# Two more pauses in the merge of the dilated branches of a hybrid decoder kernel

## The chip, the cores and the metric

One core of a Trainium2 chip runs the whole program. The metric is device time in microseconds (us) from launch to end; for the kernel before the median of three runs is given, and beside it one further execution that the hardware profiler recorded.

## The reference, cut to what matters

Two residual layers work on x of 2048 rows by 1024 columns. The change lies in layer 1, a dilated sliding-window attention with 16 heads of 64 columns. Each of its branches gives, for every query, an output `o`, the lowest score `m` and the sum `l` of its exponentials; the branches are then mixed by their softmax denominators:

```python
for o_i, m_i, l_i in branches:
    w_i = l_i * jnp.exp(m_i - big_m)
    num = num + w_i * o_i.astype(jnp.float32)
    den = den + w_i
return (num / den).astype(v.dtype)
...
oc = merge_heads(dilated_mixture(q, k, v)) * jax.nn.silu(gc)
return jnp.einsum('bse,ed->bsd', oc, w_out)
```

## The kernel before, in words

The kernel folds the three branches of the reference into two (`br` 0 and 1: near keys with a mask that counts some of them twice, and keys at stride 16). `dilated()` runs through 8 pairs of heads `p`, and in each through 4 chunks `c` of 512 queries, 2 halves of a chunk and the 2 branches: 16 units for a pair, 128 in all. A unit has scores on TensorE (L1268, tile `s_ps`), a mask and row minimum on VectorE (L1276, into `P` and the statistics `st`), exponentials on ScalarE (L1278), transposes of P on TensorE (L709, `t_ps`), their copies to SBUF on VectorE and ScalarE (L713, `pt`), and the product with the values on TensorE (L1309, `o_ps`). Scores are written four slots ahead of the rest. After the second half of a chunk ScalarE copies `o_ps` to a tile `or` (L1312); there are 11 `or` buffers, and a pair fills 8.

When a pair is complete its merge begins, spread over the units of the next pair. `merge()` returns a list of functions; entry i runs at the start of unit i + 1 after the pair's last unit, and `None` leaves a unit without a step:

- `rows`: TensorE transposes the statistics (L1334, `x_ps`), ScalarE copies them to `rt` (L1337), and SyncE's queue (SP) writes `rt` to DRAM in four transfers (`std`).
- `columns`: nine transfers on the same queue bring them back in another layout, as tile `W`.
- `weights`: nine small VectorE operations and one ScalarE exponential (L1355 `mm`, L1356 `E`, L1357, L1358 `W`, L1359 to L1361, L1363 and L1364 `w`).
- `expand(0)`, `expand(1)`: two GpSimd operations each (L1370) spread the weights into tile `X`.
- `chunk(c, br)`: TensorE spreads X over the heads (L1378, `bc_ps`, which takes one of the three PSUM buffers of the scores), VectorE multiplies `or` by it (L1379); for branch 1 GpSimd adds the two branches (L1385) and multiplies by the gate (L1386), and SP stores the result (`og`). The gate tile `sg` is loaded by branch 0's chunk.

For pairs 0 to 5, which the change touches, the list has 14 entries, for pairs 6 and 7 another. The first merge (of pair 0, run during pair 1) is called M1 below, and so on to M6; M7 is pair 6's.

The order in which each engine gets its instructions isn't the order of these lists: a scheduler of the framework sorts them by the program's order and by when it expects operands and buffers to be free, engine by engine, DMA queues included. A pause can so move instructions that the diff doesn't name. Each engine then runs its own list strictly in that order.

Of the kernel before, what the change touches and what calls it, by code (L numbers as in the profile page):

```python
# [83 lines left out]
def trunk(ctx: ExitStack, tc: tile.TileContext, A, out):  # L84
# [6 lines left out]
    def dma(o, i):  # L91
        if o.dtype == F32R:
            o = o.bitcast(F32)
        if i.dtype == F32R:
            i = i.bitcast(F32)
        return queue[0].dma_start(o, i)  # L96
# [7 lines left out]
    def dap(t, off, ap):  # L104
        return bass.AP(tensor=t.tensor, offset=t.offset + off, ap=ap)
# [1040 lines left out]
    def dilated():  # L1146
# [88 lines left out]
        def unit(p, c, br, half):  # L1235
# [81 lines left out]
            if (br, half) == (1, 1):  # L1317
                if p == 7:
                    what = merge(p, c, 1)
                elif c == 3:  # L1320
                    what = merge(p, 0, 4)
# [3 lines left out]
        def merge(p, c0, n):  # L1325

            box = {}
            R = 8 * n
            sd = st_d[p + c0]

            def rows():

                ps = x_bank("x_ps")
                TE.transpose(ps[0:4 * R, 0:128],  # L1334
                             stats[p][:, c0:c0 + n].rearrange("p c x b h t -> p (c x b h t)"), ident)
                rt = ap2.tile([128, 128], F32, tag="rt", name="rt", bufs=2)
                SC.copy(rt[0:4 * R], ps[0:4 * R, 0:128])  # L1337
                for c in range(n):
                    dma(dap(sd, c * 512, [[n * 512, 8], [128, 4], [1, 128]]), rt[32 * c:32 * c + 32])

            def columns():

                box["W"] = W = ap2.tile([128, 2, 2, 128], F32, tag="W", name="W", bufs=1)
                dma(W[0:R, :, 0], dap(sd, 0, [[128, R], [2 * R * 128, 2], [1, 128]]))
                for k in range(2):
                    for t in range(4):
                        dma(W[0:R, k, 1, 32 * t:32 * t + 32],
                            dap(sd, (2 * k + 1) * R * 128 + 128 * t, [[512, 2 * n], [32, 4], [1, 32]]))

            def weights():  # L1350
                W = box["W"][0:R]
                m, l = W[:, 0], W[:, 1]
                mm = ap2.tile([128, 128], F32, tag="mm", name="mm", bufs=1)[0:R]
                E = ap2.tile([128, 2, 128], F32, tag="E", name="E", bufs=1)[0:R]
                V.tensor_tensor(mm, m[:, 0], m[:, 1], OP.min)  # L1355
                V.tensor_tensor(E, mm[:, None, :].to_broadcast([R, 2, 128]), m, OP.subtract)  # L1356
                SC.activation(E, E, AF.Exp)  # L1357
                V.tensor_tensor(l, l, E, OP.mult)  # L1358
                V.tensor_tensor(mm, l[:, 0], l[:, 1], OP.add)  # L1359
                V.reciprocal(mm, mm)  # L1360
                V.tensor_tensor(E, E, mm[:, None, :].to_broadcast([R, 2, 128]), OP.mult)  # L1361
                ws = [ap2.tile([128, 2, 128], F32R, tag=f"w{k}", name=f"w{k}", bufs=1)[0:R] for k in range(2)]
                V.tensor_copy(ws[0], E)  # L1363
                V.tensor_tensor(ws[1], E, ws[0].bitcast(F32), OP.subtract)  # L1364
                box["w"] = ws

            def expand(br):

                for k in range(2):
                    PO.tensor_tensor(X[64 * br + 32 * k:64 * br + 32 * k + R].rearrange("p (r y) -> p r y", r=4),  # L1370
                                     box["w"][k][:, br, None, :].bitcast(F32).to_broadcast([R, 4, 128]),
                                     cc[0:R, C_M4:C_M4 + 4, None].to_broadcast([R, 4, 128]), OP.mult)

            def chunk(c, br):
                o = outs[p, br, c]
                bc = x_bank("bc_ps")
                bs = slice(64 * br, 64 * br + 64)
                TE.matmul(bc, sels[2 + c if n == 4 else 6][bs], X[bs], start=True, stop=True)  # L1378
                V.tensor_tensor(o, bc, o, OP.mult)  # L1379
                if br == 0:  # L1380
                    gates[p, c] = ap2.tile([128, 512], F32, tag="sg", name="sg", bufs=4)
                    dma(gates[p, c], sg_d[1][p, :, 512 * c:512 * c + 512])
                    return
                eng = V if (p, c) == (7, 3) else PO
                eng.tensor_tensor(o, o, outs[p, 0, c], OP.add)  # L1385
                eng.tensor_tensor(o, o, gates[p, c], OP.mult)  # L1386
                dma(og_d[1][c][p], o)

            if p < 6:
                fs = [rows, columns, None, weights, lambda: expand(0), lambda: expand(1)]  # L1390
                fs += [lambda c=c, br=br: chunk(c, br) for c in range(4) for br in range(2)]
            else:
                fs = [rows, columns] + [None] * (c0 < 3) + [weights, lambda: (expand(0), expand(1))]
                fs += [lambda c=c: (chunk(c, 0), chunk(c, 1)) for c in range(c0, c0 + n)]
            return [(i + 1, f) for i, f in enumerate(fs) if f]
# [72 lines left out]
```

## Time and profile before

| what | value |
|---|---|
| median of 3 runs | 3220.56 us (3219.57 to 3225.43) |
| the profiled execution | 3230.95 us, of it 3228.9 us span |
| TensorE busy | 3080.9 us |
| VectorE, ScalarE, GpSimd busy | 1567.0, 1282.1, 511.9 us |
| mean granted TensorE clock | 0.968 of full speed |

The span is the time from the first to the last recorded instruction. Busy time is the union of an engine's instructions; "idle before" is the time in which an engine had nothing running before an instruction, with what released it. A granted clock of 1.00 is 2.4 GHz and 0.50 is 1.2 GHz. The dilated attention lies between about 2503 and 3060 us of the span.

### The profile page before, as it was taken

What the parts mean: (1) busy time and instruction counts of PE and PEld (TensorE: products, weight loads), DVE (VectorE), ACT (ScalarE), POOL (GpSimd) and SP (SyncE); (2) the same over time, 40 slices, a digit from 0 to 9 for tenths busy, and PEclk for the clock granted to TensorE, in tenths of its full rate; (3) what the DMA queues carried; (4) which work ended last, traced back from release to release, by engine and by line L of the source; (5) the groups of instructions that cost most, each with busy time, mean ns of one, the idle gap of its engine ahead of it and who ended that gap; (6) DMA issues with size and microseconds to landing.
All of it is one profiled execution on the core that took longest, in us unless ns stands there. A gap on an engine that the chain in (4) does not pass through costs nothing. (4 is left out here: it accounts for less than half of the span.)

```text
span 3228.9 us, 60884 instructions
## 1 busy us (share of the span) xinstructions
PE 3080.9 (95%) x24252; PEld 2517.8 (78%) x24252; DVE 1567.0 (49%) x4176; ACT 1282.1 (40%) x2954; POOL 511.9 (16%) x495
## 2 busy tenths in 40 slices
PE   7999999999999999999999999999999888888898
PEld 6978889987777777777777998888888777767687
DVE  6443421001777788888554402311100777767643
ACT  5311111112766656556442321111111867766321
POOL 3200100002333200000032202220000022123321
PEclk9999999999999999999999999999999999987799
DMA  7255542216222221211352324674314655553252
GB/s 263 84 177 188 174 149 86 72 63 224 101 74 101 74 93 64 76 55 65 99 179 96 131 86 139 202 217 142 113 66 144 182 173 176 178 156 119 92 175 98
DMA packets 272309, 415.27 MB, mean 129 GB/s; under 512 B 28172, under 2 KB 155788, under 8 KB 267032
## 3 DMA queue, kind: packets, MB, share of 16 engines
q1 hardware_dynamic: 268712, 399.58, 38.6%
q0 software_dynamic: 3312, 11.80, 1.2%
q8 instruction: 190, 3.11, 0.4%
q14 instruction: 95, 0.78, 0.1%
HBM read 259.23 MB, written 152.05 MB: 127 GB/s over the span
## 5 line engine op out<-in xcount | busy, mean ns | idle before, releaser
L246 PE MATMUL pj<-hl,wh 128*128 128x512 f32 x1536 | 389.8, 396 | 0.0
L246 PE MATMUL pj<-hh,wh 128*128 128x512 f32 x1536 | 389.2, 395 | 0.0
L246 PE MATMUL pj<-hh,wl 128*128 128x512 f32 x1536 | 388.9, 395 | 0.0
L834 PE MATMUL s_ps<-K,Q 64*128 64x512 f32 (+2 forms) x1920 | 338.2, 395 | 19.0 <-DVE P L843 15.0
L709 PE MATMUL t_ps<-cc,P 64*128 64x64 f32 x5536 | 314.4, 236 | 33.5 <-DVE pt L713 20.4
L246 PEld LDWEIGHTS pj<-hl,wh 128*128 128x128 f32 x1536 | 289.4, 189 | 69.0 <-issue 0.5
L246 PEld LDWEIGHTS pj<-hh,wl 128*128 128x128 f32 x1536 | 288.6, 188 | 68.6 <-issue 0.5
L854 ACT ACTIVATE P<-P,m 128x1664 f32<-128x1664 f32 (+15 forms) x256 | 306.8, 1200 | 87.8 <-DVE m L849 87.6
L246 PEld LDWEIGHTS pj<-hh,wh 128*128 128x128 f32 x1536 | 288.1, 188 | 68.3 <-issue 1.0
L709 PEld LDWEIGHTS t_ps<-cc,P 64*128 64x128 f32 x5536 | 245.2, 143 | 114.3 <-issue 61.0
L923 PEld LDWEIGHTS o_ps<-pt,v 128*64 128x64 f32 (+1 forms) x3264 | 253.8, 158 | 87.2 <-issue 52.9
L923 PE MATMUL o_ps<-pt,v 128*64 128x128 f32 (+1 forms) x3264 | 317.1, 286 | 2.9 <-ACT pt L713 2.7
L1278 ACT ACTIVATE P<-P,st 128x256 f32<-128x256 f32 (+3 forms) x512 | 266.9, 524 | 92.0 <-DVE st L1276 90.6
L713 ACT COPY pt<-t_ps 128x512 f32<-128x512 f32 (+7 forms) x448 | 213.3, 495 | 176.2 <-PE t_ps L709 163.7
L231 DVE TENSOR_TENSOR wl<-w,wh 128x512 fp32r<-128x512 f32 (+1 forms) x128 | 84.9, 705 | 405.2 <-ACT wh L230 405.2
L713 DVE COPY pt<-t_ps 128x512 f32<-128x512 f32 (+5 forms) x384 | 229.9, 609 | 87.8 <-PE t_ps L709 69.0
L1276 DVE CUSTOM_DVE_ANT_0 P<-s_ps,band 128x256 f32<-128x256 f32 (+3 forms) x512 | 204.6, 448 | 111.4 <-PE s_ps L1268 108.3
L834 PEld LDWEIGHTS s_ps<-K,Q 64*128 64x128 f32 x1920 | 202.4, 192 | 60.6 <-DVE P L843 24.9
L1268 PE MATMUL s_ps<-K,Q 64*128 64x256 f32 (+2 forms) x1536 | 193.6, 339 | 12.9 <-DVE st L1276 11.5
L1309 PE MATMUL o_ps<-pt,v 128*64 128x128 f32 x2272 | 178.6, 298 | 9.4 <-DMA v<-v 3.5
L267 ACT ACTIVATE hi<-pj 128x512 fp32r<-128x512 f32 x80 | 47.8, 597 | 350.0 <-PE pj L246 329.8
L840 DVE CUSTOM_DVE_ANT_0 P<-s_ps,F 128x512 f32<-128x512 f32 (+1 forms) x192 | 121.4, 669 | 109.7 <-PE s_ps L834 108.9
(245 smaller groups left out, 4371.6 us busy)
## 6 DMA issues: line engine op xcount, KB each, us to landing
Q<-q SPq DMA_DIRECT2D x31, 1024.0 KB
ada<-ada_w SPq DMA_DIRECT2D x96, 256.0 KB
sg<-t2k SPq DMA_DIRECT2D x64, 256.0 KB
xt<-x SPq DMA_DIRECT2D x32, 512.0 KB
w<-w SPq DMA_DIRECT2D x64, 256.0 KB
q<-yb SPq DMA_DIRECT2D x64, 256.0 KB
x<-x SPq DMA_DIRECT2D x28, 512.0 KB
w<-w0b SPq DMA_DIRECT2D x56, 256.0 KB
```

The lines of the kernel that those rows point to most:

```text
L231: V.tensor_tensor(wl[:, 2 * q:2 * q + 2, :n], w[:, :, :n], wh[:, 2 * q:2 * q + 2, :n].bitcast(F32), OP.subtract)
L246: TE.matmul(ps, a[:, d, 128 * j:128 * j + 128], b[:, d, :], start=n == 0, stop=n == 23)
L709: TE.transpose(ps[k][:, n], b[rs], ident[rs, rs])
L713: last_flip[eng is SC] = f(pt[:, :len(blocks), 64 * k:64 * k + 64], ps[k][:, :len(blocks)])
L834: TE.matmul(ps[j][:, :n], queries[p, i // 4][hs, a, qs], keys[p][b][hs, c0:c0 + n], start=first, stop=a == 1)
L840: V.tensor_tensor_reduce(P[:, c0:c0 + n], ps[j][:, :n], forgets[p][j][:, c0:c0 + n], 1.0, 3.0e38, OP.add, OP.min, m)
L854: SC.activation(P, P, AF.Exp, bias=lows[j], scale=-1.0, accum_out=lt[:, j, col:col + 1])
L923: TE.matmul(o[:, cs], values[p][:, b, hs], pts[j, b], start=b == 0, stop=b == i)
L1268: TE.matmul(ps[hh][:, o:o + N], q[hs, qs], t["keys"](kk[hs]), start=k == 0, stop=k == 2)
L1276: V.tensor_tensor_reduce(P[:, hh, j, :n], ps[hh][:, o:o + n], m[:, m.shape[1] - n:], 1.0, 3.0e38, OP.add, OP.min, mn)
L1278: SC.activation(P[:, hh, j, :n], P[:, hh, j, :n], AF.Exp, bias=mn, scale=-1.0, accum_out=l)
L1309: TE.matmul(to, values[p, br][:, kc, hs], where[hh, j, o, kc], start=k == 0, stop=k == n - 1)
```

## The change

For pairs 0 to 5 the list of the merge gets two more `None`. The one behind the first `None` sets `weights` and all that follows one unit later; the one after `expand(1)` sets the chunks one unit later again, two in all. The list has 16 entries in place of 14. Nothing is computed otherwise.

```diff
             if p < 6:
-                fs = [rows, columns, None, weights, lambda: expand(0), lambda: expand(1)]
+                fs = [rows, columns, None, None, weights, lambda: expand(0), lambda: expand(1), None]
                 fs += [lambda c=c, br=br: chunk(c, br) for c in range(4) for br in range(2)]
```

What the scheduler makes of it, at three places. First TensorE in M1, in the stretch after the transposes that stand beside the statistics (`s_ps` scores, `t_ps` transposes, `o_ps` products with the values, `bc_ps` the spread weights). Before:

```order
L709 MATMUL t_ps<-cc,P 128x64 x16
L1309 MATMUL o_ps<-pt,v 64x4x32 x8
L709 MATMUL t_ps<-cc,P 128x64 x16
L1309 MATMUL o_ps<-pt,v 64x128 x7
L1378 MATMUL bc_ps<-X,sel_1700 128x512
L1268 MATMUL s_ps<-K,Q 128x256 x12
```

With the change, from the same row on:

```order
L709 MATMUL t_ps<-cc,P 128x64 x16
L1268 MATMUL s_ps<-K,Q 128x256 x12
L1309 MATMUL o_ps<-pt,v 64x4x32 x8
L709 MATMUL t_ps<-cc,P 128x64 x16
L1268 MATMUL s_ps<-K,Q 128x384 x6
L1309 MATMUL o_ps<-pt,v 64x128 x8
L1378 MATMUL bc_ps<-X,sel_1700 128x512
```

Two groups of scores that stood behind the first `bc_ps` now stand ahead of it. All rows ahead of this place are the same; M2 to M6 change in the same way.

Second VectorE in M1, at the end of `weights` (`w` are its two results, L1276 the masks of the scores):

```order
 L713 COPY pt<-t_ps 128x8x64
 L1361 TENSOR_TENSOR E<-E,mm 32x256
-L1363 CAST w_25768<-E 32x256
-L1364 TENSOR_TENSOR w_25769<-E,w_25768 32x256
+L1363 CAST w_25818<-E 32x256
+L1276 ISA P,st<-s_ps,band 128x256
+L1276 ISA st 128x1
+L1364 TENSOR_TENSOR w_25819<-E,w_25818 32x256
+L1276 ISA P,st<-s_ps,band 128x256
```

The first operation of `weights`, L1355, keeps its place on VectorE in all six merges (the same row number in both lists); only the end of `weights` moves, by one mask of a score, and the first L1379, which stood some rows behind it, moves further down.

Third SP's queue between M1 and M2 (`og_3` the last result of M1, `v` values for a later pair, `std` the statistics of M2):

```order
 L96 DMA og_3_79<-or 128x512
-L96 DMA K<-k_67 128x1024
-L96 DMA Q<-q_66 128x2048
-L96 DMA sg<-sg_71 128x512
-L96 DMA Q<-q_66 128x2048
 L96 DMA v<-v_69 128x16x128
-L96 DMA v<-v_69 32x4x128
 L96 DMA std_89<-rt 8x4x128 x4
```

The store of M1's last result now stands right ahead of the large load of `v`, which stands ahead of M2's `std`; one small load of `v` that stood there now comes behind. It is the same ahead of M3 to M6; ahead of M1 nothing moves.

## Rows read from the trace of the kernel before

**Rows 1.** The page's busy time of each engine: time, share of the span, instructions.

```profile
PE 3080.9 (95%) x24252; PEld 2517.8 (78%) x24252; DVE 1567.0 (49%) x4176; ACT 1282.1 (40%) x2954; POOL 511.9 (16%) x495
```

**Rows 2.** Windows from one transpose of the statistics to the next, M4 to M6.

```profile
core 0: us, PE busy (x) PEld busy (x) DVE busy (x) ACT busy (x) POOL busy (x), PEclk, DMA share, GB/s
...
2749.00:2810.00 61.00, 53.90 (x776) 44.39 (x772) 48.53 (x174) 44.29 (x152) 14.62 (x12) 0.92 0.56 174
2810.00:2880.00 70.00, 61.22 (x777) 49.92 (x773) 48.25 (x172) 44.98 (x152) 14.56 (x12) 0.83 0.50 153
2880.00:2948.00 68.00, 59.65 (x769) 48.19 (x765) 47.44 (x171) 45.56 (x152) 14.57 (x12) 0.85 0.45 134
```

**Rows 3.** Waits of PE, 2560 to 2950 us: who, for whom, total us, times, longest.

```profile
PE t_ps L709 <- DVE pt L713: 19.7, 8, 4.5
PE bc_ps L1378 <- POOL X L1370: 10.1, 6, 2.7
...
PE t_ps L709 <- ACT pt L713: 5.0, 6, 1.6
```

**Rows 4.** Waits of DVE in the same stretch.

```profile
DVE or L1379 <- PE bc_ps L1378: 23.4, 14, 3.1
DVE mm L1355 <- DMA W<-std: 23.3, 6, 5.7
```

**Rows 5.** Timeline of M1: start, duration, instruction, idle before it.

```profile
2576.89 0.28 DVE L1355 TENSOR_TENSOR mm<-W 32x128 f32<-32x128 f32 x1 [2.96 <-DMA W<-std]
...
2578.64 0.71 PE L709 MATMUL t_ps<-cc,P 64*128 64x64 f32 x15 [2.40 <-DVE pt L713]
...
2582.49 0.71 PE L709 MATMUL t_ps<-cc,P 64*128 64x64 f32 x15 [1.64 <-ACT pt L713]
...
2583.43 4.51 POOL L1370 TENSOR_TENSOR X<-w,cc 32x512 fp32r<-32x512 f32 x4 [80.69 <-DVE w L1363]
...
2586.88 0.79 PE L1378 MATMUL bc_ps<-X,sel 64*128 64x512 f32 x1 [2.67 <-POOL X L1370]
...
2587.71 0.69 DVE L1379 TENSOR_TENSOR or<-bc_ps,or 128x512 f32<-128x512 f32 x1 [2.78 <-PE bc_ps L1378]
```

**Rows 6.** Timeline from the end of M1 to the start of M2.

```profile
2611.32 0.40 PE L1378 MATMUL bc_ps<-X,sel 64*128 64x512 f32 x1
...
2616.34 0.32 SPq L96 DMA_DIRECT2D og<-or  x1
...
2618.79 0.96 PE L1268 MATMUL s_ps<-K,Q 64*128 64x256 f32 x12
...
2623.54 5.97 SPq L96 DMA_DIRECT2D v<-v  x2
...
2625.60 0.33 PE L1334 MATMUL x_ps<-cc,st 128*128 128x128 f32 x1
...
2627.71 0.26 ACT L1337 COPY rt<-x_ps 128x128 f32<-128x128 f32 x1
...
2629.60 2.91 SPq L96 DMA_DIRECT2D std<-rt  x4
2632.56 1.61 SPq L96 DMA_DIRECT2D v<-v  x3
2634.88 5.82 SPq L96 DMA_DIRECT2D W<-std  x9
```

**Rows 7.** Windows at low granted clock, in M1 to M6 (columns as in Rows 2).

```profile
2584.00:2592.00 8.00, 5.33 (x46) 4.04 (x44) 3.98 (x13) 2.04 (x8) 4.53 (x5) 0.57 0.50 164
...
2838.00:2854.00 16.00, 16.00 (x108) 12.02 (x108) 9.17 (x29) 8.99 (x29) 5.07 (x4) 0.50 0.40 122
2905.00:2921.00 16.00, 15.84 (x109) 11.89 (x109) 10.20 (x36) 9.81 (x31) 5.08 (x4) 0.50 0.37 118
```

**Rows 8.** Timeline, PE: the wait for X in M5.

```profile
2835.56 0.50 PE L1378 MATMUL bc_ps<-X,sel 64*128 64x512 f32 x1 [1.46 <-POOL X L1370]
```

**Rows 9.** Timeline: an `or` copy that waits for GpSimd, and a weight split in M7.

```profile
2607.47 0.59 ACT L1312 COPY or<-o_ps 128x512 f32<-128x512 f32 x1 [1.49 <-POOL or L1385]
...
2957.81 0.69 DVE L609 TENSOR_TENSOR wo<-raw,wo 128x512 fp32r<-128x512 f32 x1 [1.08 <-ACT wo L608]
```

## The prediction

> **What bounds the kernel now.** I read the busy times first. TensorE is busy 3080.9 us of the span and no other engine half of it [rows 1], so a change pays only by what it takes off TensorE's idle time or its slow time. The windows from one transpose of the statistics to the next come second [rows 2]: in a merge TensorE is busy about 54 of 61 us, and in M5 and M6, at a lower mean clock, the same work takes 70 and 68 us. So each merge holds some 7 us of idle time, and the last two cost 7 to 9 us more through the clock.
>
> The waits third. In the six merges TensorE stands 19.7 us for VectorE's copies of transposes and 10.1 us, once in each merge, for GpSimd's X [rows 3]. VectorE stands 23.3 us, once in each merge, for W to land, and 23.4 us for the spread weights [rows 4]. The timeline of M1 puts them in order [rows 5]. VectorE reaches L1355 before W has landed and stands 2.96 us; the copies queued behind it are late, and TensorE stands 2.40 us. A second stall of 1.64 us on a copy follows. Then GpSimd starts X, and TensorE, which has the first `bc_ps` next in its list, stands 2.67 us; VectorE behind it stands 2.78 us for that product. For those 2.7 us both engines stand still although scores could be computed.
>
> **The change, part by part.** *The pause ahead of `weights`.* By its name it should take away the wait for W. The lists say that it doesn't: L1355 keeps its place on VectorE in all six merges, and TensorE's rows up to that stall are the same. I cost it at nothing by itself: the 23.3 us of VectorE [rows 4] and what hangs on them stay. Its ends are the 19.7 us of TensorE [rows 3] if the place meant nothing, and nothing; the unchanged list decides for the latter.
>
> *The pause ahead of the chunks.* Twelve and six scores now stand ahead of the first `bc_ps`. Twelve take 0.96 us at full clock [rows 6], six wide ones about as long, and the wait for X averages 10.1 / 6 = 1.7 us [rows 3]: the cover is about as long as the wait. At most 10.1 us go. But the twelve scores stand ahead of the products with the values and need score buffers that VectorE empties only after its first stall; I put back about 2 us for that over the six merges, which is the size of the second stalls (1.64 us in M1, [rows 5]) traded against the scores that now fill them. That term is **-8 us**, between -10 and -3. VectorE's waits for the product lie beside TensorE's and aren't counted again. The same number of products, multiplications and stores is issued as before; moved by two units, they fall into the same kind of work and cost nothing by themselves.
>
> *What the pause pushes on SP's queue.* The last store of a merge, `og_3`, now stands right ahead of the large `v` load, and that one ahead of the next merge's `std`. In M1 the last `bc_ps` starts at 2611.32 and `og_3` is issued at 2616.34, 5.0 us later, the rest of the chain (VectorE, two GpSimd operations) between them [rows 6]. With the change the last `bc_ps` stands behind the scores that begin at 2618.79 and end at 2619.75, so `og_3` is issued near 2624.8, and the `v` load 0.32 us later, at 2625.1 in place of 2623.54: 1.6 us late. One small `v` load, 1.61 / 3 = 0.54 us, no longer stands ahead of `std`. So `std`, whose data are ready at 2627.97, is issued 1.1 us later at most, and W lands as much later. VectorE may reach the last multiplication earlier than in this chain, so I take 0.8 us; every such microsecond is added to the first stall of VectorE and TensorE. It hits M2 to M6: 5 x 0.8 = **+4 us**, between -2.7 (the store is done in time, the small load is gone: 5 x 0.54) and +7.5.
>
> *M7.* Its list isn't changed, but one more weight split stands ahead of the end of its `weights`: **+0.7 us** [rows 9].
>
> *The clock.* TensorE's granted clock falls to half in every merge. In M1 it is 0.57 from 2584 to 2592 us, after the first stalls, which stay. In M5 and M6 it is 0.50 for 16 us, with TensorE busy all the time [rows 7]; in M5 that stretch begins after the wait of 1.46 us for X [rows 8], in a merge whose clock had already come back from the first fall. M5 and M6 take 70 and 68 us against 61 for M4 [rows 2]: about 15 us together. If these second falls come from the wait for X, they go. But the profiled execution stands 10.4 us above the median of the runs (3230.95 against 3220.56), which I read as most of these 15 us: the usual run holds only some 4.6 us of them. So the term is -15 against the profiled execution and **-4.6** against the median, between -10 and +7 (one long stretch more or fewer).
>
> The Trainium skill, in TensorE: Matmul & The Clock Gate, section Part 1: The HAM clock gate, says that the window in which TensorE's activity is judged runs freely, so that the place of a fall shifts from run to run. By that rule the long stretches in M5 and M6 would be an accident of that execution rather than the work of the wait for X, and the sum would lack its clock term. No row here decides: one execution shows them, two merges of six.
>
> *The sum.* Against the profiled execution: 3230.95 - 8 + 4 + 0.7 - 15 = 3212.7. Against the median: 3220.56 - 8 + 4 + 0.7 - 4.6 = 3212.7. The forecast is **3213 us**, 0.24% faster. About 0.2%, 6.4 us, is what a measurement of this kernel can tell from no change, so it lies just beyond that.
>
> **The rivals.** *The gain is given back within the merge, or the clock gives nothing.* TensorE's wait for X ends, but the next thing late is the same stall one row further: VectorE comes to the copies of the transposes after four masks more than before, so the product with the values waits for them; or the `or` copy waits; or the long slow stretches, two in six merges of one execution, aren't the work of the wait for X. A pair fills 8 of 11 `or` buffers, so the fourth copy of the next pair needs one that GpSimd's addition of chunk 0 frees, and that addition now comes two units later. An `or` copy already waits 1.49 us for it once [rows 9]; one such wait in each of six merges is up to 9 us on ScalarE, and on TensorE what of it the buffered products don't cover. With half the gain gone (-4), +4 on SP's queue, +0.7 and no clock term the time is 3221; with the full -8 and no clock term it is 3217. For it speaks that three engines are each busy 70 to 88% in a merge [rows 2]; against it that scores are written four slots ahead. Chance 0.33.
>
> *The other side: SP's queue makes it slower.* If `og_3` comes 2.5 us later than `v` could go, as when the chain through VectorE and GpSimd meets a busy VectorE, `std` is 2 us late in five merges: +10. From 1.6 us a merge on (8 / 5) this outweighs the -8. Longer first stalls also make a long slow stretch likelier; one more is +7 [rows 2]. The time is 3220.6 - 8 + 10 + 0.7 + 7 = 3230. For it speaks that the move stands in the list and that W is late already; against it that the chain of 5.0 us [rows 6] includes VectorE's own delay. Chance 0.22.
>
> *The larger gain.* The first stall doesn't grow, the full 10.1 us go and no merge has a long slow stretch: 3220.6 - 10.1 + 0.7 - 9 = 3202. Chance 0.12, on the same side as the forecast.
>
> **How the numbers follow.** The forecast has 0.33. Faster by over 0.2% (under 3214.1) takes 0.29 of it, the larger gain's 0.12 and 0.03 of the give-back: 0.44. Within 0.2%: 0.30 of the give-back and the forecast's other 0.04: 0.34. Slower by over 0.2% (over 3227): the queue's 0.22. The range of 8 in 10 goes from 3198, past the larger gain, to 3229, short of the queue's full price.
>
> **What would show it.** Right: no wait of `bc_ps` for X in M1 to M6 (10.1 us before, now under 2), VectorE's wait for W of the old size in M1 and up to 1 us longer in M2 to M6, `og_3` issued right ahead of the `v` load about a microsecond before the statistics' transpose, and 60 us or less from merge to merge. Wrong: the wait for W gone (then the pause ahead of `weights` does work, and the gain is over 20 us), or new waits of TensorE for ScalarE's `or` copies, or a first stall longer by 2 us, or granted clocks of 0.50 for 16 us in more merges than two.

## The result, and the profile after

| what | before | after |
|---|---|---|
| median of 4 runs each | 3220.07 us (3219.32 to 3225.43) | 3197.09 us (3194.13 to 3200.87) |
| ratio | 1 | 0.9924, 95% interval [0.9901, 0.9947] |
| profiled execution | 3230.95 us, span 3228.9 us | 3197.35 us, span 3195.4 us |

The change makes the kernel 23 us faster, 0.76%. The direction was forecast; the size was not: 3213 us was said, with a range down to 3198.

The busy line of the profile after, to be read beside [rows 1]:

```profile
PE 3052.8 (96%) x24252; PEld 2498.1 (78%) x24252; DVE 1567.6 (49%) x4176; ACT 1281.4 (40%) x2954; POOL 511.2 (16%) x495
```

TensorE runs the same 24252 instructions and is busy 28 us less, 21.7 of them in the six merges. That is no work saved; it is the same work at a higher clock. The windows from one transpose of the statistics to the next show where. First the kernel after, M4 to M6 and then all six merges (columns as in [rows 2]):

```profile
2738.81:2795.73 56.92, 51.54 (x772) 42.65 (x770) 48.76 (x172) 44.33 (x152) 14.45 (x12) 0.97 0.59 186
2795.73:2856.66 60.93, 52.44 (x772) 43.46 (x770) 48.29 (x172) 44.44 (x152) 14.47 (x12) 0.92 0.57 177
2856.66:2915.56 58.90, 52.34 (x771) 43.44 (x770) 47.63 (x171) 45.45 (x153) 14.46 (x12) 0.94 0.49 153
2560.70:2915.56 354.86, 314.87 (x4616) 260.75 (x4615) 289.86 (x1025) 268.80 (x909) 86.77 (x72) 0.94 0.56 174
```

and the six merges of the kernel before:

```profile
2564.46:2948.44 383.98, 336.56 (x4616) 275.89 (x4615) 288.30 (x1025) 269.35 (x909) 87.35 (x72) 0.90 0.53 163
```

The six merges are 383.98 - 354.86 = 29.1 us shorter with the same 4616 matmuls. TensorE's idle time falls from 383.98 - 336.56 = 47.4 us to 40.0, that is by 7.4; its busy time falls by 21.7. A mean clock of 0.90 with two levels, 1.00 and 0.50, means that (1 - 0.90) / 0.5 = 20% of the time, some 77 us, was at the lower one; 0.94 means some 43 us. M5 and M6, the 70 and 68 us of [rows 2], are now 61 and 59, and M4 fell from 61 to 57. Each merge has one low stretch left, which begins in the stall or right behind it. In the kernel before, M5 and M6 have a second one of 16 us behind the wait for X [rows 7]; with the change no merge has a second. M2 as an example: its first broadcast starts at 2643.72, and the clock is at 1.00 over the 20 us around and behind it:

```profile
2642.00:2662.00 20.00, 19.24 (x273) 15.53 (x272) 18.18 (x55) 15.49 (x50) 7.25 (x7) 1.00 0.45 153
```

Of the 33.6 us between the two profiled executions, another 3.8 lie ahead of the first merge, in code that the change doesn't touch.

The waits of TensorE in the six merges (who, for whom, total, times, longest), beside [rows 3]:

```profile
PE s_ps L1268 <- DVE st L1276: 20.3, 32, 2.0
PE t_ps L709 <- DVE pt L713: 18.4, 6, 5.2
PE t_ps L709 <- ACT pt L713: 1.1, 2, 0.5
```

The wait for X, 10.1 us before, is gone. The wait for VectorE's copies is as it was (19.7), and the scores now stand 20.3 us for score buffers that VectorE empties. In the kernel before that was 8.4:

```profile
PE s_ps L1268 <- DVE st L1276: 8.4, 18, 0.9
```

VectorE's waits in the same stretch, beside [rows 4]:

```profile
DVE mm L1355 <- DMA W<-std: 24.1, 6, 6.4
DVE or L1379 <- PE bc_ps L1378: 15.1, 19, 1.5
...
DVE W L1358 <- DMA W<-std: 5.6, 5, 1.3
```

The wait for W is as it was: 24.1 us, 23.3 before, and 5.6 us (4.3 before) for its last parts one operation later. The pause ahead of `weights` didn't take it away. SP's queue from the end of M1 to the start of M2, beside [rows 6] (start and duration of the issue; the transpose of the statistics starts at 2619.90):

```profile
2618.15 0.32 SPq L96 DMA_DIRECT2D og<-or  x1
2618.56 0.39 SPq L96 DMA_DIRECT2D v<-v  x1
2622.42 3.11 SPq L96 DMA_DIRECT2D std<-rt  x4
2625.63 1.40 SPq L96 DMA_DIRECT2D v<-v  x3
2628.24 5.82 SPq L96 DMA_DIRECT2D W<-std  x9
```

`og_3` now stands right ahead of the large `v` load, as the lists said, but that load takes 0.39 us to issue. The 5.97 us of two `v` loads in [rows 6] were mostly the small one behind it. One by one (shortest, median and longest issue in ns; first and last start), the two of the kernel before are

```profile
L96 SPq DMA_DIRECT2D v<-v x2: 371/2082/3794, 2623.5 to 2625.7; - x2
```

The one that starts at 2625.7 and ends with the 5.97 us takes 3.79 us; it is the small one, and the change moves it behind `std`. ScalarE's copy of the statistics ends at 2622.39 and `std` goes out at 2622.42, without delay, and W's transfers start 8.34 us after the transpose in place of 9.28.

### The profile page after: what moved, and what is told of

Read it like the earlier page. It is cut to its first block, busy times and chain, and to the rows that moved or that the text cites. A ratio compares the mean times of both kernels' runs of the same rounds, so it can differ in the third digit from the quotient of the medians.

```text
span 3195.4 us, 60888 instructions
## 1 busy us (share of the span) xinstructions
PE 3052.8 (96%) x24252; PEld 2498.1 (78%) x24252; DVE 1567.6 (49%) x4176; ACT 1281.4 (40%) x2954; POOL 511.2 (16%) x495
## 5 line engine op out<-in xcount | busy, mean ns | idle before, releaser
L709 PE MATMUL t_ps<-cc,P 64*128 64x64 f32 x5536 | 306.4, 234 | 29.5 <-DVE pt L713 19.1
L1276 DVE CUSTOM_DVE_ANT_0 P<-s_ps,band 128x256 f32<-128x256 f32 (+3 forms) x512 | 204.4, 446 | 98.6 <-PE s_ps L1268 95.3
L268 DVE SCALAR_TENSOR_TENSOR lo<-pj,hi 128x512 fp32r<-128x512 f32 x80 | 55.2, 690 | 246.0 <-ACT hi L267 233.8
```

Source lines behind the costliest of these rows:

```text
L709: TE.transpose(ps[k][:, n], b[rs], ident[rs, rs])
L1276: V.tensor_tensor_reduce(P[:, hh, j, :n], ps[hh][:, o:o + n], m[:, m.shape[1] - n:], 1.0, 3.0e38, OP.add, OP.min, mn)
```

## The experiments

All runs stand beside runs of the kernel before on the same chip, whose medians there were 3223.8 to 3228.1 us. "Six merges" runs from M1's transpose of the statistics to M7's. Idle is its length less TensorE's busy time; dummy work counts as busy. The last three columns are of one profiled execution, which can lie some 6 us from its kernel's median (3188.11 us in wq_fill28).

| kernel | median us (runs) | ratio to before | six merges | TensorE busy, idle | clock |
|---|---|---|---|---|---|
| before_again | 3230.56 (1) | | 380.68 | 335.10, 45.6 | 0.89 |
| one_pause | 3210.98 (12) | 0.9959 [0.9944, 0.9974] | 365.72 | 317.94, 47.8 | 0.93 |
| two_ahead | 3201.93 (6) | 0.9926 [0.9901, 0.9951] | 356.38 | 317.60, 38.8 | 0.93 |
| change_again | 3197.71 (6) | 0.9917 [0.9899, 0.9935] | 355.67 | 318.73, 36.9 | 0.93 |
| w_two_queues | 3192.62 (4) | 0.9904 [0.9871, 0.9936] | 346.83 | 311.21, 35.6 | 0.96 |
| no_w_change | 3167.51 (4) | 0.9817 [0.9787, 0.9846] | | | 1.00 (M2 to M6) |
| no_w_before | 3175.9 (4) | 0.9842 [0.9812, 0.9872] | | | 0.98 (M2 to M6) |
| warm | 3199.28 (4) | 0.9918 [0.9886, 0.995] | 354.15 | 330.76, 23.4 | 0.99 |
| wq_warm | 3194.39 (4) | 0.9899 [0.9863, 0.9934] | 350.20 | 338.31, 11.9 | 1.00 |
| wq_fill28 | 3194.35 (6) | 0.9901 [0.9883, 0.992] | 347.79 | 326.25, 21.5 | 0.99 |
| wq_fill16 | 3195.68 (6) | 0.9908 [0.9889, 0.9927] | 349.26 | 321.90, 27.4 | 0.97 |
| weights_late | 3191.23 (6) | 0.9896 [0.9875, 0.9917] | 348.90 | 315.31, 33.6 | 0.95 |
| weights_later | 3185.44 (6) | 0.9878 [0.9852, 0.9903] | 339.24 | 308.04, 31.2 | 0.98 |

### Was the low clock an accident of the one execution?

The kernel before, profiled once more, without an edit.

> The kernel before, unchanged, profiled once more. If the long slow stretches of M5 and M6 (16 us at a granted clock of 0.50) are the work of the wait for X, they stand in the same merges or at least in two of six again, and the six merges take about 384 us from the first transpose of the statistics to the seventh (before: 383.98). If they were an accident of one execution, no merge has one, the six take about 370 us, and the time is near 3210 to 3220.

The six merges, and two low stretches in M2 and M6:

```profile
2567.22:2947.90 380.68, 335.10 (x4617) 275.62 (x4615) 287.98 (x1025) 269.09 (x909) 87.45 (x72) 0.89 0.53 164
...
2652.46:2658.46 6.00, 5.86 (x38) 4.84 (x40) 3.32 (x13) 2.08 (x8) 2.59 (x4) 0.50 0.31 130
2908.89:2916.89 8.00, 8.00 (x53) 5.85 (x52) 5.35 (x18) 5.04 (x17) 2.55 (x2) 0.50 0.25 69
```

Neither forecast holds as it was put. No merge takes 70 us here; all six take 61 to 65. But the mean clock is 0.89, some 84 us at the lower level against 77, and the busy time is within 2 us of the first execution's. The long stretches have moved: M3's now lasts some 17 us, and M2, M5 and M6 have a second one. In the two executions five merges of twelve have a second fall, each within about 2 us of the first broadcast, which had to wait for X; in the two executions of the change and in two_ahead below, where nothing waits for X, none of eighteen has one.

What low clock costs can be read from the same merge in the two executions. M5 takes 70 us at a mean clock of 0.83 [rows 2], and here

```profile
2818.64:2882.89 64.25, 56.15 (x771) 46.29 (x769) 47.89 (x172) 44.61 (x152) 14.63 (x12) 0.89 0.54 167
```

That is 24 and 14 us at the lower level, and the merge is 5.7 us longer with the 10 us more. M2, M3, M4 and M6 go the same way: the execution with the lower clock is the longer one.

The sum agrees in these two executions, but both took about 3231 us. The seventeen runs of the same kernel beside this one lie between 3212.8 and 3238.4 us, at granted clocks of 0.965 to 0.974 over the whole run; the three fastest have 0.973 and 0.974, the slowest 0.965. So the sum differs between runs, too.

The Trainium skill (TensorE: Matmul & The Clock Gate, Part 1: The HAM clock gate) says that the window of the clock's monitor runs freely, so that the place of a change differs from run to run. The places do differ between these two executions; that such a window is the reason, no run here shows.

### Which of the two pauses works?

One pause alone, ahead of the chunks (a single one ahead of `weights` was not run; its instruction lists are the same, names apart), and both behind `expand(1)`:

```diff
-fs = [rows, columns, None, None, weights, lambda: expand(0), lambda: expand(1), None]
+fs = [rows, columns, None, weights, lambda: expand(0), lambda: expand(1), None]         # one_pause
+fs = [rows, columns, None, weights, lambda: expand(0), lambda: expand(1), None, None]   # two_ahead
```

> One pause in place of two (behind expand(1) alone; the pause ahead of weights left out). The instruction lists of TensorE, VectorE and ScalarE are then those that a single pause ahead of weights gives, too: only the unit at which the chunks start counts, one later than before, one earlier than in the change. Theory A (chunks start later, so the wait for X is filled): 12 scores of about 1 us stand ahead of the first spread product; of the 10.1 us wait for X some 4 us stay, idle time of TensorE is between the two kernels, time 3204 to 3212. Theory B (both pauses are needed, the order of scores decides): no gain, 3216 to 3222. Theory C (the first moved score group does all): as the change, 3194 to 3201.

> Two pauses ahead of the chunks and none more ahead of weights: the lists of TensorE, ScalarE and SP's queue are the change's, only the end of weights on VectorE stands as before. Theory A (the chunks' start is all): as the change, 3194 to 3201. Rival (the pause ahead of weights does its part, by the end of weights and X starting later or by less work ahead of the late scores): at least 5 us slower than the change, 3202 to 3212.

The six merges of one_pause:

```profile
2560.79:2926.51 365.72, 317.94 (x4617) 264.90 (x4615) 290.55 (x1025) 269.11 (x909) 86.77 (x72) 0.93 0.54 170
```

TensorE's waits in them:

```profile
PE s_ps L1268 <- DVE st L1276: 17.8, 27, 2.2
PE t_ps L709 <- DVE pt L713: 14.1, 6, 4.0
PE bc_ps L1378 <- POOL X L1370: 13.8, 6, 3.8
```

In two_ahead, with only the end of `weights` in another place on VectorE than in the change:

```profile
2564.23:2920.61 356.38, 317.60 (x4617) 262.81 (x4615) 289.91 (x1025) 268.92 (x909) 86.72 (x72) 0.93 0.56 174
```

two_ahead equals the change within noise: its ratio is 0.9926 against 0.9924, each to about 0.0025 (8 us), and its six merges are within 2 us of the change's. So the unit at which the chunks begin counts, and no worth of the place of `weights` is seen. In microseconds it lies at the edge between its two forecasts, since the kernel before was slower beside it, too (3224.88). The first unit of delay brings about half of the gain, and not through the wait for X: that *grows*, from 10.1 to 13.8 us, and the idle time stays at 47.8 us (47.4 before). So the time of one_pause falls into the range of theory A by luck, for its mechanism doesn't hold. The whole 18 us by which its merges are shorter between the profiled executions are busy time, with the clock at 0.93 in place of 0.90; by the medians the kernel is 14 us faster. Where X is waited for, second falls are back, in two merges of six (M3, M6). The second unit takes idle time, 47.8 to 38.8.

### Is it the wait for W that makes both the idle time and the low clock?

First the path of W is made shorter: half of the `std` and half of the eight small W transfers go on GpSimd's queue.

```diff
+queue[0] = PO if p < 6 and c % 2 else nc.sync    # std of row block c
...
+queue[0] = PO if p < 6 and t % 2 else nc.sync    # part t of W
```

> The change, and half of the transfers of the statistics (two of four to DRAM, four of nine back) on GpSimd's queue instead of SP's. Theory A (the first stall of VectorE is the landing of W, and SP issues its transfers one after the other): W is complete 2 to 4 us earlier, VectorE's wait for W falls from 24 us over six merges to under 12, TensorE's stall on its copies with it, and the low clock that follows the stall gets shorter: 3172 to 3188. Rival (GpSimd's queue issues and lands slower, or L1355, which the scheduler puts three rows earlier, waits as long): 3192 to 3203.

VectorE's and TensorE's longest waits in its six merges:

```profile
DVE mm L1359 <- DMA W<-std: 25.6, 6, 5.7
...
PE t_ps L709 <- DVE pt L713: 21.1, 7, 4.9
```

The scheduler, seeing W earlier, set the first operation on W three rows earlier on VectorE, so it waits as long as ever (25.6 us; in this kernel the line is L1359). The 5.6 us for the last parts of W are gone, TensorE's wait for score buffers falls from 20.3 to 13.2 us, and the merges are 8 us shorter; the time is the rival's. Next the transfers of W are left out of M2 to M6, in the change and in the kernel before:

```diff
-for c in range(n):                               # rows: std
+for c in range(n if p in (0, 6, 7) else 0):
...
+if 0 < p < 6:                                    # columns: W of pair 0 again
+    box["W"] = first_W[0]
+    return
```

> The change, with the transfers of std and W left out in M2 to M6: those merges take the W tile of pair 0 again, so they compute other weights, but VectorE never waits for W there. Stall theory (VectorE, waiting about 4 us in order for W, starves TensorE of emptied score and transpose buffers, and the idle stretch that this makes is what TensorE's clock falls after): in M2 to M6 the 18 us of PE waits for t_ps<-DVE pt are under 5, granted clock 0.98 or more from merge to merge instead of 0.94, each of these intervals 52 to 54 us instead of 58.9, the kernel about 3165 to 3175 us. Rival (the clock falls by itself in the finely interleaved work of a merge, whatever waits there): clock stays at 0.94 to 0.95, only some of the 6.7 us of idle per merge goes, 55 to 57 us each, the kernel 3180 to 3190.

> The same transfers left out of the kernel before (no added pause). Stall theory: without the W wait the weights are ready some 4 us earlier, so the first broadcast no longer waits for X either; both idle stretches and the low clock after them go in M2 to M6, and this kernel comes within 4 us of the change without W waits. Rival (the pause itself is worth its gain in the clock, because the chunks lie at a better place of the row): it stays 15 to 25 us above the change without W waits, with the X wait gone or not.

M2 to M6 of the change without W's transfers:

```profile
2622.89:2887.30 264.41, 249.63 (x3848) 207.32 (x3846) 234.95 (x842) 222.29 (x756) 67.95 (x56) 1.00 0.63 193
```

of the kernel before without them:

```profile
2625.70:2891.25 265.55, 251.64 (x3847) 210.00 (x3846) 232.09 (x831) 221.93 (x755) 67.58 (x56) 0.98 0.64 192
```

and the same five merges of the change and of the kernel before as they are:

```profile
2619.90:2915.56 295.66, 260.72 (x3847) 216.18 (x3846) 240.78 (x854) 224.11 (x758) 72.29 (x60) 0.94 0.56 176
```

```profile
2625.60:2948.44 322.84, 284.02 (x3847) 232.50 (x3846) 239.91 (x854) 225.06 (x758) 72.80 (x60) 0.89 0.53 162
```

In M2 to M6 a merge takes 52.9 us and 53.1 us without the transfers, against 59.1 and 64.6 with them, so there the change is worth next to nothing. But more goes with the transfers than VectorE's wait. Nothing ties `weights` to the statistics any more, and the scheduler makes the X of M2 ahead of M2's transpose of the statistics, which starts at 2622.89 in the change and at 2625.70 in the kernel before (the first GpSimd row of each, without the transfers):

```profile
2613.20 2.14 POOL L1376 TENSOR_TENSOR X<-w,cc 32x512 fp32r<-32x512 f32 x2 [1.75 <-PE bc_ps L1384]
...
2605.10 2.21 POOL L1376 TENSOR_TENSOR X<-w,cc 32x512 fp32r<-32x512 f32 x2
```

So the five intervals hold 56 of their 60 GpSimd operations, and M1's holds 16 in place of 12. With M1 all 72 are there, in the change and in the kernel before without the transfers:

```profile
2561.37:2887.30 325.93, 303.19 (x4617) 251.30 (x4615) 289.78 (x1025) 267.52 (x909) 86.70 (x72) 0.99 0.61 188
...
2558.34:2891.25 332.91, 307.70 (x4616) 255.03 (x4615) 289.54 (x1025) 267.48 (x909) 86.44 (x72) 0.97 0.61 186
```

These six merges are 28.9 us shorter than the change's and 51.1 us shorter than those of the kernel before. Of the 7.0 us between the two, 5.8 lie in M1, where both still wait for W (61.5 and 67.4 us). The medians stand 8.4 us apart, and all four runs of one lie below all four of the other: the 4 us of the stall theory are exceeded, the rival's 15 to 25 us aren't reached. So most of what the change saves hangs on the late W: the wait, the late X, the second idle stretch and the low clock behind it. A worth of the pause of up to 8 us by itself isn't excluded, and these runs don't tell VectorE's standing still apart from the mere lateness of the weights.

### Does the low clock cost the time, or the stall?

TensorE's idle stretch behind the wait for W is filled with transposes of the identity into the idle broadcast bank, right ahead of the transposes that wait: 48 in the change (warm), then 64, 28 and 16 in the variant with two queues.

```diff
+def warm():
+    ps = x_bank("wm_ps")
+    for _ in range(48):
+        TE.transpose(ps[:, 0:128], ident, ident)
```

> The change, with 48 transposes of the identity into the idle broadcast bank put right ahead of the transposes at which TensorE waits for VectorE in a merge (about 2.9 us of work by the 0.06 us of a 128-column matmul; nothing reads them). Stall theory: the work lies inside an idle stretch of 2.8 us, so it costs under 1 us per merge, and with no idle stretch but the shorter one behind it (2.0 us) the clock stays at 1.00 in most merges: low clock halves or better, merges 54 to 57 us each, the kernel 3175 to 3190 us. Rival (the clock falls for another reason, or the second stretch of 2.0 us is enough for it): same low clock as the change, the kernel 3194 to 3205.

> The variant with std and W on two queues, whose idle of 4 us per merge lies in one place, and 64 such transposes (about 3.9 us) right ahead of the transposes that wait there. Stall theory: hardly an idle stretch is left, clock 0.98 or more from merge to merge, merges 53 to 55 us, the kernel 3168 to 3180 us, below all versions so far that compute the same. Rival: no change against that variant without them, 3190 to 3196 us.

The dummies in M3 of wq_warm, in order of time, and what comes behind them:

```profile
2684.55 7.21 PE L1357 MATMUL wm_ps<-cc 128*128 128x128 f32 x64
2691.69 0.71 PE L709 MATMUL t_ps<-cc,P 64*128 64x64 f32 x16
```

The clock did stay at 1.00 from merge to merge in wq_warm, and had a mean of 0.99 in warm. But I had priced a transpose at 0.06 us; it takes 7.21 / 64 = 0.113, so 64 overfilled a stretch of 4 us and 48 one of 2.8 us, and no time was gained (3194 against 3193 us, 3199 against 3197). With the number put right:

> The variant with 64 added transposes, with 28 of them instead. There the 64 took 7.2 us, 0.113 us each, in an idle stretch of 4 us, so they held the clock at 1.00 and delayed the merge by some 3 us. 28 take 3.2 us, inside the stretch. Stall theory: nothing is delayed (the merge loses the 36 x 0.113 = 4.1 us, of which what the W wait still holds stays, some 0.8 us) and the clock stays at 1.00: intervals of 58.4 - 3.2 = about 55 us, the six 331 us, the kernel 3172 to 3178 us. Rival (the dummies only moved time, the clock falls again as soon as any idle stretch is left): low clock of 3 to 5 us per merge as without dummies, the kernel 3186 to 3194 us.

> The same with 16 transposes (1.8 us), which leave about 2.3 us of the idle stretch open. Stall theory, if a stretch of about 2 us is short enough for the clock (the change's chunk waits of 0.4 to 0.5 us, and waits of up to 1.4 us in the variant without W transfers, made no fall): 1.00 in most merges and 3172 to 3180 us, as with 28. If it is long enough for it: low clock in most merges, the kernel 3184 to 3192 us.

The stall in M3 of wq_fill28, in order of time:

```profile
2683.06 3.28 PE L1357 MATMUL wm_ps<-cc 128*128 128x128 f32 x28
...
2686.26 0.27 PE L709 MATMUL t_ps<-cc,P 64*128 64x64 f32 x1
...
2687.04 0.71 PE L709 MATMUL t_ps<-cc,P 64*128 64x64 f32 x15 [0.51 <-DVE pt L713]
```

Its M3 as a whole:

```profile
2673.54:2731.99 58.45, 53.92 (x799) 44.80 (x797) 47.26 (x171) 45.25 (x153) 17.91 (x18) 1.00 0.58 181
```

M3 without dummies, in w_two_queues:

```profile
2671.37:2729.43 58.06, 51.39 (x771) 42.70 (x769) 47.60 (x171) 45.32 (x153) 17.73 (x18) 0.97 0.59 186
```

Here 28 dummies fit (0.51 us of idle time is left behind them), the clock is 1.00 through M3, and M3 isn't shorter: 58.45 against 58.06 us. M1 and M5 are alike. 28 and 16 give 3194 and 3196 us, against 3193 without. My stall theory had the idle stretch right as what the clock falls after, and was wrong on the price: a *short* low stretch right behind the stall, some 3.5 us in a merge whose mean clock is 0.97, costs nothing that can be measured. A longer one is another matter. In M2 of wq_fill28 the clock fell in spite of the dummies. First that merge, then M2 of w_two_queues:

```profile
2613.25:2673.54 60.29, 56.48 (x799) 46.95 (x797) 48.26 (x172) 44.41 (x152) 17.94 (x18) 0.94 0.57 181
...
2612.84:2671.37 58.53, 51.97 (x771) 42.91 (x769) 48.46 (x172) 44.41 (x152) 17.76 (x18) 0.97 0.60 187
```

M6 has 57.88 us at 1.00 with the dummies and 59.69 at 0.94 without; M4 shows no difference (57.89 at 0.97, 57.72 at 0.94). The change's own two executions speak for a price as well: M4 takes 56.92 us at 0.97 in the first, and in change_again

```profile
2733.07:2793.43 60.36, 54.30 (x772) 44.89 (x770) 49.02 (x172) 44.65 (x152) 14.46 (x12) 0.92 0.56 175
```

Each of these is one merge of one execution. Over the six merges of wq_fill28, TensorE's own work takes 326.25 - 168 x 0.113 = 307.3 us, 3.9 less than in w_two_queues; its idle time and the dummies take 21.5 + 19.0 = 40.5 us, 4.9 more than the 35.6 there. In sum, what the clock gave came back as waiting. I read it so that VectorE, which stood for 4 us, then has a backlog that sets the pace; that reading is argued from these sums and not tried by itself.

> The change as it is, once more beside the variants: by its earlier runs 3194 to 3201 us, six merges of 353 to 360 us in sum, clock 0.93 to 0.95 in them. If the gain in clock was luck of one chip or hour, as the prediction took the low clock of the kernel before to be, it comes out above 3205 us here; by the stall theory it stays where it was, some 25 us below the kernel before.

The change once more: 3197.71 us, merges of 355.67 us, 0.93. Its gain is no luck of one run.

### Can the wait be taken away without leaving work out?

On two queues, the first operation on W is tied behind VectorE's last transpose copy and `weights` is listed two units later (weights_late) or three (weights_later); the chunks begin where the change has them, or one unit later.

```diff
-fs = [rows, columns, None, None, weights, lambda: expand(0), lambda: expand(1), None]
+fs = [rows, columns, None, None, None, None, weights, lambda: (expand(0), expand(1))]         # late
+fs = [rows, columns, None, None, None, None, None, weights, lambda: (expand(0), expand(1))]   # later
...
+with tc.issue_after(last_flip[False].ins):
     V.tensor_tensor(mm, m[:, 0], m[:, 1], OP.min)
```

> The variant with std and W on two queues, with the first operation on W put some 3 us later among VectorE's (6 rows: four score copies with their reads and two transpose copies ahead of it now), the chunks where the change has them. VectorE theory (the merge is as long as VectorE's work and its stand-still for W; the low clock right behind the stall lies beside VectorE's catching up and costs nothing): the W wait falls from 25.6 us to under 8 in the six merges, each is some 3 us shorter, the six 327 to 332 us, the kernel 3170 to 3178 us. Rival 1 (the stall only moves: X, made 3 us later, is waited for by TensorE ahead of the first broadcast): an X wait of 2 to 3 us per merge and 3186 to 3194 us. Rival 2 (TensorE's clock sets the merge, the stall is only what starts the low stretch): with no idle stretch of over 2 us the clock is 0.99 and the time below 3175, as in the first case, but merges in which the clock still falls stay at 58 us.

> The same one unit later: the first operation on W 11 rows later than in the variant on two queues (some 5 us), and the chunks one unit later than in the change. VectorE theory: the W wait is gone but for 3 us, nothing waits for X, the six merges 318 to 326 us, as in the runs without W transfers (52.9 us each), the kernel 3162 to 3172 us. Rival (a third unit of delay runs the chunks into the next merge's first units and its gated rows, or the output buffers): 3180 to 3192 us, with new waits for or buffers or of the last chunks.

The waits in weights_late:

```profile
PE s_ps L1268 <- DVE st L1276: 21.2, 29, 2.4
PE bc_ps L1386 <- POOL X L1378: 9.4, 6, 1.9
...
DVE mm L1361 <- DMA W<-std: 9.1, 5, 3.2
```

and in weights_later:

```profile
PE o_ps L1309 <- ACT or L1312: 9.4, 6, 1.6
PE bc_ps L1386 <- POOL X L1378: 5.4, 2, 2.7
...
DVE or L1387 <- PE bc_ps L1386: 20.1, 21, 1.8
...
DVE mm L1361 <- DMA W<-std: 0.7, 1, 0.7
```

weights_late is the case of rival 1: the wait for W falls from 25.6 to 9.1 us, and a wait of TensorE for X of 9.4 us takes its place, so nothing is gained over two queues (3191 and 3193 us). weights_later has no wait for W, and 5.4 us for X; with 3185 us and 0.9878 it has the lowest median of the kernels that leave no work out, though its interval still overlaps theirs. Against the forecast of 3162 to 3172 it stops short, and its time is the rival's: with the chunks three units late TensorE's products wait 9.4 us for ScalarE's `or` copies, for which nothing waits in the six merges of the change, and VectorE stands 20.1 us for the broadcasts.

## Why the prediction was wrong in size

- *The pause ahead of `weights`, 0.* Right: VectorE's wait for W is 24.1 us (23.3), and two_ahead, which has no such pause, equals the change within noise.
- *The pause ahead of the chunks, -8.* Right in sum, by another account. X is no longer waited for, -10.1. I put back 2 us for scores that wait for VectorE; that wait grew by 11.9 us (8.4 to 20.3), while TensorE's waits for the copies of transposes fell (VectorE's from 19.7 to 18.4, ScalarE's from 5.0 to 1.1). Idle time as a whole: -7.4.
- *SP's queue, +4.* Wrong in mechanism. The step "`std` ... is issued 1.1 us later at most" took the large `v` load as the one that held the queue. It was the small load behind it (3.79 us), which the change moves behind `std`; `std` goes out when its data are ready, and the term is about nothing in place of +4. VectorE's wait for W grew by 0.8 us, in six merges together. The rival that made the kernel slower through this queue falls with it.
- *M7, +0.7.* From M7's transpose to the end of the span it is 279.8 us, 280.5 before: not to be seen.
- *The clock, -4.6 against the median.* This is the step that failed: "the profiled execution stands 10.4 us above the median of the runs, which I read as most of these 15 us: the usual run holds only some 4.6 us of them". Its condition held: "If these second falls come from the wait for X, they go", and in the change no merge has a second fall. But I counted as low clock that could go only the two long stretches in M5 and M6, took the falls in the other merges as part of the first stalls, "which stay", and then took most of the two for an accident. before_again has no merge of 70 us, but second falls in three merges and the same low clock in sum, 0.89. Between the first two profiled executions the change took some 34 us of low clock (77 less 43) and 21.7 us of busy time; between the other two, before_again and change_again, busy time falls by 16.4 us and idle time by 8.7. Against the median, 23 us in all less 7.4 of idle time leaves about 15 us for the clock, three times the 4.6. The profiled execution may well hold more low clock than the usual run (0.968 over the whole run, against a median of 0.970 in the seventeen runs beside before_again); what failed is that the usual run's share was put at 4.6.

What would show it: no wait for X (right), a wait for W of the old size (right), `og_3` ahead of `v` and 1.75 us ahead of the transpose (right), 60 us or less from merge to merge (four of six; 60.4 and 60.9 are the others). None of the signs of being wrong came. The rival of the larger gain, 3202 us with a chance of 0.12, came nearest: all of the wait for X gone and no long slow stretch left.

What stays open: why one unit of delay brings the clock back sooner although X is waited for longer (13.8 us). The runs show that it does, from 77 and 84 us at the lower level in the six merges to some 51. They also show that long low stretches lengthen a merge and that a short one right behind the stall doesn't; they don't show what makes a stretch in a merge long or short.

## What to carry to other kernels

A wait that one engine can't step around (here VectorE's for W, 4 us a merge) costs more than its length: its followers start late, and TensorE's clock falls behind the idle stretches. So look for the wait that all the others hang on by leaving its transfer out once; that run gives a bound on what a cure further down the chain can be worth. But look what else moved: here `weights` and X went ahead of the merge as well, so the bound is a loose one. And before a slow stretch in one profile is called an accident, a second profile of the same kernel is to be compared in sums over the stage, not place by place, together with the granted clocks of the other runs.

## What the runs showed of the hardware

- The places of low clock differ between two executions of one kernel (the longest merge was 69.9 us in one and 65.0 in the other) where its sum over six merges is about the same (mean clock 0.90 and 0.89). Over more runs the sum differs, too: 0.965 to 0.974 over whole runs of 3238.4 to 3212.8 us.
- Of these kernels, a second fall of the clock in a merge came in five merges of twelve in the kernel before and in two of six in one_pause, each time near a first broadcast that waited for X, and in none of eighteen in the change and two_ahead, where nothing waits for X.
- TensorE's clock stayed at 1.00 through 7.21 us in which it ran only transposes of a constant, in the place of an idle stretch of 4 us behind which it falls otherwise. Such a transpose of 128 x 128 fp32 takes 0.113 us at full clock, about twice what I had assumed.
- Right behind the stall a short low stretch cost nothing: M3 took 58.06 us with it (mean clock 0.97) and 58.45 us without. Longer ones did in most places: M4 of the change took 56.92 us at 0.97 and 60.36 us at 0.92.
